# Two layers of a hybrid decoder on one core: another pacing of modulations and transposes, two heads' late rows in products of 512 and 256 columns, and another form of the last norm's factors

## The chip, the core and the metric

One Trainium2 chip, one of its cores. The time is what the device takes for one execution of the whole program, in microseconds; a kernel's time is the median of its runs. All weights come from the chip's own memory during the execution.

## What is computed

The reference, cut to what matters here. Two layers: a retention mixer (8 heads) with a SwiGLU feed-forward, then a short convolution mixer with a second SwiGLU, 256 tokens of width 2048, all in float32.

```python
for i in range(DEPTH):                                   # DEPTH = 2
    mod = (c_act @ w_mod[i] + b_mod[i])[:, None, :]      # one conditioning vector
    sh1, sc1, g1, sh2, sc2, g2 = jnp.split(mod, 6, axis=-1)
    h = rms_norm(x, norm1_g[i]) * (1.0 + sc1) + sh1
    y = retention_mixer(h, ...) if i == 0 else short_conv_mixer(h, ...)
    x = x + g1 * y
    h = rms_norm(x, norm2_g[i]) * (1.0 + sc2) + sh2
    x = x + g2 * swiglu(h, ffn_w_in[i], ffn_w_out[i])    # D_FF = 5632
return rms_norm(x, final_g)

def retention_mixer(h, cos, sin, w_in, w_out):
    q, k, v, g = jnp.split(h @ w_in, ...)                # q, k rotated by position
    o = rms_norm(chunked_gated_linear_attention(q, k, v, log_a))
    return (jax.nn.silu(g) * o) @ w_out
```

## The kernel before

**Products.** TensorE (PE) multiplies rounded operands. Each float32 weight tile is split in two rounded parts, `hi` (cast on ScalarE, ACT, L416) and `lo` (the rest, a subtraction on VectorE, DVE, L419), and so is each activation row. A product is then hi·hi + hi·lo + lo·hi. Three helpers write it out:

- `product` (L469, L472): weights stand still, and the activation's both parts, 512 columns, go past `hi`; a second matmul sends the rounded part, 256 columns, past `lo`. A result column group takes a whole bank of PSUM, with the two halves added later on DVE.
- `packed` (L531 to L533): the same in three matmuls of 256 columns, whose sum stands in half a bank.
- `thrice` (L482 to L484): activations stand still and the weights, 512 columns, go past, three matmuls for each 128 tokens. The retention values, the feed-forward's main part and, by `sevens`, a form of it with seven instead of eight block products use it.

**Weights.** One sequence of 1 MB pieces (`raw`) holds all weights in the order of use. `fetch` loads them (L377) into a ring of four buffers, which the modulation's pieces share (L315), on SyncE's queue (SP). `prepare` splits a piece; the parts go into five places of 1024 columns, so TensorE's weights are made some steps ahead of their use.

**Modulations.** A column of 128 values of `mod` is one multiply with a running sum on DVE over a 1 MB piece of `w_mod` (L323, at low priority), and a small step on GpSimd (POOL, L328 to L333). 160 of them are spread over the program by `paced`: after each step of the products it compares the count so far with the table `plan_mod`, whose pairs are (product units so far, modulations due by then). A unit is 128 rows by 128 columns of weights. Up to unit 2048 runs the retention with its output; up to 2688 the first feed-forward's first input part; up to 3008 its first output part; up to 3776 its second input part; 5184 is the end of the convolution mixer.

**Heads.** They run in the order 4, 0, 2, 1, 5, 3, 6, 7. Of some heads a part of the rows (`ks`) has already been multiplied in the start phase and is held in SBUF (`ahead`): of heads 0 and 1 the first ten of sixteen rows, of heads 2 and 3 the first thirteen. `pair(head, i)` makes q (i = 0), k (1) and the gate (2): the late rows go through `packed`, and L1111 adds the held part. Heads 5, 6 and 7 (`SIDE_BY_SIDE`) have nothing held and use `product` for q and k.

**Transposes.** A head's outputs are made while the next head's projections run: `mixed` leaves three steps (`outputs(0)`, `last_outputs`, `ends`) in a list, and `ticked` calls each after so many product units, by `STEPS`. `ends` transposes the normed outputs `o` (L1073) with TensorE (L1084).

**The gated units' banks.** After a group of sevens `mixed_sums` (L1208 to L1212) adds four banks of sums into SBUF; the next group of products waits for these banks.

**The end.** The last output products leave token-major banks; `added` multiplies by the gate, adds the residual and takes the sum of squares on ACT; `stored` finishes the final norm: the mean (L1446, DVE), the power −1/2 (L1450, POOL), the scaling (L1453 ACT, L1455 and L1457 DVE) and the stores (L1459).

**What sets the order.** TensorE's instructions stand as the program writes them. Those of DVE, ACT and POOL are put into one order for each engine by the framework's scheduler, by priorities, when the program is built; each engine then works its list off in that order and waits on semaphores.

Of the kernel before, what the change touches and what calls it, by code (L numbers as in the profile page):

```python
# [13 lines left out]
AF = mybir.ActivationFunctionType  # L14
# [3 lines left out]
P = 128  # L18
# [29 lines left out]
MOD_LEAD = 64  # L48
MOST = 0.08
MOD_PRIO = -300  # L50
STEPS = (8, 8, 20)
RAW_BUFS = 4
PLACES = 5
FETCHED, PLAIN, WARM, ADDED = 2, 3, (5, 0, 0, 0, 0, 0, 0, 8), ()
SIDE_BY_SIDE = (5, 6, 7)
LEFT, ENDS, EARLIER = 8, 2, 120

Q0, K0, V0, G0 = 0, HEADS * DK, 2 * HEADS * DK, 2 * HEADS * DK + HEADS * DV
# [203 lines left out]
def trunk(ctx: ExitStack, tc: tile.TileContext, x_in, c_in, pos_in, w_mod, cols_in, gain_in, tab_in, w_all, out):  # L262
# [12 lines left out]
    def tmp(tag, shape=(P, S), dtype=F32, pool=work, bufs=None):  # L275
        return pool.tile(list(shape), dtype, tag=tag, name=name(tag), bufs=bufs)
# [63 lines left out]
    todo.reverse()  # L340
    first = RET_SPANS[0].n * FIRST_KS
    early = sum(g.n * len(g.ks) for g in RET_SPANS)
    plan_mod = [(early, 0), (1024, 28), (1984, 72), (2688, 84), (3008, 96), (3776, 106), (5184, n_mod)]
    units, allowed = [0], [0.0]

    def paced(n):
# [112 lines left out]
    def product(g, act, base=0, before=None, banks=None, last=True):  # L459

        fresh = not banks
        banks = banks or [bank() for _ in g.cols]
        for k in g.ks:
            if before:
                before(k)
            h = act[k - base]
            for c, pt in zip(g.cols, banks):
                hi, lo = take(g, k, c)
                nc.tensor.matmul(  # L469
                    pt, hi, h, start=fresh and k == g.ks[0], stop=False, skip_group_check=True  # L470
                )
                nc.tensor.matmul(  # L472
                    pt[:, 1, :], lo, h[:, 0, :], start=False, stop=last and k == g.ks[-1], skip_group_check=True
                )
            ticked(len(g.cols))
            paced(len(g.cols))
        return banks
# [241 lines left out]
    with ExitStack() as inner:  # L719
# [374 lines left out]
        def pair(head, i):  # L1094

            g = RET_HEADS[head][0][i]
            if not g.ks:
                return [ahead[head, n] for n in ((i,) if i < 2 else (2, 3))]
            if i < 2 and head in SIDE_BY_SIDE:
                both = tmp("qs", (P, 2, S), pool=rp, bufs=1)  # L1100
                for j, pt in enumerate(product(g, h)):
                    summed(pt, both[:, j])
                return [both]
            sums = packed(g, h)
            for j, pt in enumerate(sums):
                key = (head, i + j)
                if key in tag_of:
                    free.append(tag_of.pop(key))
                if key in ahead:
                    s = tmp("qs", (P, 2, S), pool=rp, bufs=1)  # L1110
                    nc.vector.tensor_tensor(s, ahead[key], pt, op=ALU.add)  # L1111
                    sums[j] = s
            return sums
# [306 lines left out]
    def gated(t, c, v, priority):  # L1420

        xs = at(xt[t], c)
        with tc.high_priority(offset=priority):
            nc.vector.tensor_tensor(v, v, gate_of[c], op=ALU.mult)
            nc.vector.tensor_tensor(xs, xs, v, op=ALU.add)

    def added(t, c, pt, last):

        u, xs = tmp("u512", (P, DV), pool=mpool, bufs=3), at(xt[t], c)
        nc.vector.tensor_tensor(u, pt, gate_of[c], op=ALU.mult)  # L1430
        nc.vector.tensor_tensor(xs, xs, u, op=ALU.add)
        if not last:
            return
        nc.scalar.activation(u, xs, AF.Square, accum_out=total[:, t, c : c + 1])
        if c < 3:
            nc.vector.tensor_tensor(xs, xs, gain_of[c], op=ALU.mult)
        if c == 2:
            some = sums_of[:, t : t + 1]
            nc.gpsimd.tensor_tensor(some, total[:, t, 0:1], total[:, t, 1:2], op=ALU.add)
            nc.gpsimd.tensor_tensor(some, some, total[:, t, 2:3], op=ALU.add)  # L1440
            nc.gpsimd.tensor_scalar(some, some, 1.0 / D, EPS, op0=ALU.mult, op1=ALU.add)

    def stored(t):

        r = tmp("rs", (P, 2), bufs=4)[:, 0:1]
        nc.vector.tensor_scalar(  # L1446
            r, total[:, t, 3:4], 1.0 / D, sums_of[:, t : t + 1], op0=ALU.mult, op1=ALU.add
        )
        root = tmp("rs", (P, 2), bufs=4)[:, 0:1]
        nc.gpsimd.tensor_tensor(root, r, half[:, 0:1], op=ALU.pow)  # L1450
        for i in range(2):
            a, b = at(xt[t], 2 * i), at(xt[t], 2 * i + 1)
            nc.scalar.activation(a, a, AF.Identity, scale=root)  # L1453
            if i:
                nc.vector.scalar_tensor_tensor(b, b, root, gain_of[3], op0=ALU.mult, op1=ALU.mult)  # L1455
            else:
                nc.vector.tensor_scalar(b, b, root, None, op0=ALU.mult)  # L1457
            o = slice(2 * DV * i, 2 * DV * (i + 1))
            nc.sync.dma_start(out[t, :, o], xt[t][:, o])  # L1459

    def last_output(part, c, groups, act, base):
# [24 lines left out]
        for (t, j), v in extra.items():  # L1486
            gated(t, c + j, v, MOD_PRIO)
            if part:
                xs, n = at(xt[t], c + j), c + j
                nc.scalar.activation(v, xs, AF.Square, accum_out=total[:, t, n : n + 1])  # L1490
                nc.vector.tensor_tensor(xs, xs, gain_of[n], op=ALU.mult)

    for part in range(2):
# [53 lines left out]
```

## Time and profile before

| | |
|---|---|
| three runs | 2565.79, 2567.32, 2568.79 us |
| the profiled execution | 2568.4 us, its span 2566.6 us |
| granted TensorE clock in it | 0.998 |
| weights and tables loaded | 685.11 MB, 268 GB/s over the span |

The span goes from the first to the last instruction; the 1.8 us beside it lie around the program. In the rows a line number names the line of the code, `bank` is PSUM, `raw` a loaded piece, and a matmul of 128x512 has 512 columns going past. A matmul's time in a row is longer than the distance to the next one's start, since they overlap; what a matmul costs is read from the starts.

### The profile page before, as it was taken

Reading aid. Unit: us, or ns where it says so; the run is one execution under the profiler, and the core shown is the slowest. Engines: PE = TensorE matmul, PEld = TensorE weight load, DVE = VectorE, ACT = ScalarE, POOL = GpSimd, SP = SyncE. Lnnn points to the kernel's source line nnn. Section 1 sums busy time; section 2 is a strip of 40 time slices with the busy share of each in tenths; the row PEclk is TensorE's granted clock in tenths of the full one; section 3 lists DMA queues with packets and bytes.
Section 4 is the critical chain, followed back from the end, with each engine's and each line's share of the span. In section 5 each row is a group of like instructions: output and inputs, shape, how many; then the busy total and the mean of one; then the engine's idle time right before and its main releaser. Section 6 shows DMA issues by size and latency. Waiting matters only on the chain.

```text
span 2566.6 us, 34867 instructions
## 1 busy us (share of the span) xinstructions
PE 2543.9 (99%) x13330; PEld 2186.1 (85%) x13330; DVE 2334.6 (91%) x2925; ACT 1346.1 (52%) x1789; POOL 178.4 (7%) x232
## 2 busy tenths in 40 slices
PE   8999999999999999999999999999999999999998
PEld 6898888888889888888888898888998888888887
DVE  7989999898899999889999888888989999999988
ACT  5544443454456555345555454444565555555554
POOL 0000111011111010000000111000000000000001
PEclk9999999999999999999999999999999999999999
DMA  9987889888876667866668878878846465555653
GB/s 398 390 331 263 309 321 340 334 300 308 329 278 234 231 261 285 322 245 227 248 230 301 302 282 309 330 292 299 317 159 214 180 229 212 181 214 182 228 197 131
DMA packets 96696, 689.48 MB, mean 269 GB/s; under 512 B 10744, under 2 KB 12168, under 8 KB 13456
## 3 DMA queue, kind: packets, MB, share of 16 engines
q1 hardware_dynamic: 96528, 687.25, 72.1%
q8 instruction: 104, 1.70, 0.3%
q14 instruction: 64, 0.52, 0.1%
HBM read 685.11 MB, written 2.11 MB: 268 GB/s over the span
## 4 chain that ended last, share of the span: by engine, by line
PE 90%; DVE 6%; DMA 2%; issue 1%; ACT 1%; ACTq 0%; SPq 0%; POOLq 0%; POOL 0%; DVEq 0%
PE bank L469 20%; PE bank L482 17%; PE bank L484 17%; PE bank L483 17%; PE bank L472 11%; DVE lo L419 2%; DMA raw<-w_all 1%; PE bank L533 1%; PE bank L664 1%; PE bank L532 1%; PE bank L666 1%; PE bank L665 1%; PE bank L531 1%; DVE raw L795 1%; DVE raw L323 1%
## 5 line engine op out<-in xcount | busy, mean ns | idle before, releaser
L416 ACT CAST hi<-raw 128x1024 fp32r<-128x1024 f32 (+1 forms) x981 | 990.5, 1020 | 932.8 <-PE bank L484 361.8
L419 DVE TENSOR_TENSOR lo<-raw,hi 128x1024 fp32r<-128x1024 f32 (+1 forms) x981 | 1143.9, 1181 | 148.3 <-ACT hi L416 143.3
L482 PE MATMUL bank<-hi,h 128*128 128x512 f32 x1540 | 602.7, 391 | 1.1 <-DVE u L1212 1.0
L483 PE MATMUL bank<-lo,h 128*128 128x512 f32 x1540 | 600.9, 390 | 0.1
L484 PE MATMUL bank<-hi,h 128*128 128x512 f32 x1540 | 600.8, 390 | 0.0
L323 DVE SCALAR_TENSOR_TENSOR raw<-raw,cb 128x2048 f32<-128x2048 f32 x160 | 365.9, 2287 | 28.9 <-DMA raw<-w_mod 28.6
L484 PEld LDWEIGHTS bank<-hi,h 128*128 128x128 f32 x1540 | 289.3, 188 | 61.2
L482 PEld LDWEIGHTS bank<-hi,h 128*128 128x128 f32 x1540 | 289.5, 188 | 59.6 <-DVE u L1212 1.9
L483 PEld LDWEIGHTS bank<-lo,h 128*128 128x128 f32 x1540 | 289.6, 188 | 58.4 <-DVE lo L419 0.8
L469 PE MATMUL bank<-h,hi 128*128 128x512 f32 x928 | 323.0, 391 | 0.0
L469 PE MATMUL bank<-mid,hi 128*128 128x512 f32 x920 | 319.4, 390 | 0.0
L472 PE MATMUL bank<-h,lo 128*128 128x256 f32 x928 | 261.3, 282 | 0.0
L472 PE MATMUL bank<-mid,lo 128*128 128x256 f32 x920 | 259.6, 282 | 0.0
L469 PEld LDWEIGHTS bank<-h,hi 128*128 128x128 f32 x928 | 174.1, 188 | 36.9
L469 PEld LDWEIGHTS bank<-mid,hi 128*128 128x128 f32 x920 | 172.7, 188 | 35.8
L472 PEld LDWEIGHTS bank<-h,lo 128*128 128x128 f32 x928 | 175.7, 189 | 0.3
L472 PEld LDWEIGHTS bank<-mid,lo 128*128 128x128 f32 x920 | 174.2, 189 | 0.1
L469 PE MATMUL bank<-rm,hi 128*128 128x512 f32 x496 | 172.5, 391 | 0.0
L472 PE MATMUL bank<-rm,lo 128*128 128x256 f32 x496 | 140.0, 282 | 0.0
L482 PE MATMUL bank<-hi,mid 128*128 128x512 f32 x297 | 116.0, 391 | 0.0
L484 PE MATMUL bank<-hi,mid 128*128 128x512 f32 x297 | 115.9, 390 | 0.0
L483 PE MATMUL bank<-lo,mid 128*128 128x512 f32 x297 | 115.7, 390 | 0.0
(281 smaller groups left out, 3430.4 us busy)
## 6 DMA issues: line engine op xcount, KB each, us to landing
raw<-w_all SPq DMA_DIRECT2D x456, 1024.0 KB, 5.0
raw<-w_mod SPq DMA_DIRECT2D x192, 1024.0 KB, 6.3
x<-x_in SPq DMA_DIRECT2D x4, 512.0 KB, 5.4
out<-xt SPq DMA_DIRECT2D x4, 512.0 KB, 3.0
decay<-tab_in SPq DMA_DIRECT2D x8, 128.0 KB, 5.3
x<-gate_row SPq DMA_DIRECT2D x2, 512.0 KB, 4.8
last_gain<-gain_in SPq DMA_DIRECT2D x1, 1024.0 KB
cols<-cols_in SPq DMA_DIRECT2D x1, 152.0 KB, 8.2
```

Of the source, the lines that this page charges most:

```text
L323: nc.vector.scalar_tensor_tensor(raw, raw, 1.0, cb, op0=ALU.mult, op1=ALU.mult, accum_out=total)
L416: nc.scalar.copy(hi[:, o], raw[:, o])
L419: nc.vector.tensor_tensor(lo, raw, hi.bitcast(F32), op=ALU.subtract)
L469: nc.tensor.matmul(pt, hi, h, start=fresh and k == g.ks[0], stop=False, skip_group_check=True)
L472: nc.tensor.matmul(pt[:, 1, :], lo, h[:, 0, :], start=False, stop=last and k == g.ks[-1], skip_group_check=True)
L482: nc.tensor.matmul(o, hi, w_hi, start=first, stop=False)
L483: nc.tensor.matmul(o, hi, w_lo, start=False, stop=False)
L484: nc.tensor.matmul(o, lo, w_hi, start=False, stop=last)
L531: nc.tensor.matmul(pt, hi, h[:, 0, :], start=first, stop=False, skip_group_check=True)
L532: nc.tensor.matmul(pt, hi, h[:, 1, :], start=False, stop=False, skip_group_check=True)
L533: nc.tensor.matmul(pt, lo, h[:, 0, :], start=False, stop=last, skip_group_check=True)
L664: nc.tensor.matmul(pt, hi, high, start=k == 0, stop=False, skip_group_check=True)
```

## The change

```diff
-STEPS = (8, 8, 20)
+STEPS = (8, 8, 24)
-SIDE_BY_SIDE = (5, 6, 7)
+SIDE_BY_SIDE, HELD_SIDE_BY_SIDE = (5, 6, 7), (1, 3)
...
-    plan_mod = [(early, 0), (1024, 28), (1984, 72), (2688, 84), (3008, 96), (3776, 106), (5184, n_mod)]
+    plan_mod = [(early, 0), (1024, 28), (1984, 72), (2688, 80), (3008, 96), (3776, 102), (5184, n_mod)]
...
+            if i < 2 and head in HELD_SIDE_BY_SIDE:
+                key = (head, i)
+                both = tmp("qs", (P, 2, S), pool=rp, bufs=1)
+                pts = product(g, h)
+                for j, pt in enumerate(pts):
+                    nc.vector.tensor_tensor(both[:, j], ahead[key][:, j], pt[:, 0, :], op=ALU.add)
+                    nc.vector.tensor_tensor(both[:, j], both[:, j], pt[:, 1, :], op=ALU.add)
+                free.append(tag_of.pop(key))
+                return [both]
...
-        nc.scalar.activation(u, xs, AF.Square, accum_out=total[:, t, c : c + 1])
-        if c < 3:
-            nc.vector.tensor_tensor(xs, xs, gain_of[c], op=ALU.mult)
+        sq = tmp("u512", (P, DV), pool=mpool, bufs=3)
+        nc.scalar.activation(sq, xs, AF.Square, scale=D**-0.5, accum_out=total[:, t, c : c + 1])
+        dst = xs if c < 3 else u
+        nc.vector.tensor_tensor(dst, xs, gain_of[c], op=ALU.mult)
+        gained[t] = dst
...
-            nc.gpsimd.tensor_scalar(some, some, 1.0 / D, EPS, op0=ALU.mult, op1=ALU.add)
+            nc.gpsimd.tensor_scalar(some, some, EPS, None, op0=ALU.add)
...
-        r = tmp("rs", (P, 2), bufs=4)[:, 0:1]
-        nc.vector.tensor_scalar(
-            r, total[:, t, 3:4], 1.0 / D, sums_of[:, t : t + 1], op0=ALU.mult, op1=ALU.add
-        )
         root = tmp("rs", (P, 2), bufs=4)[:, 0:1]
-        nc.gpsimd.tensor_tensor(root, r, half[:, 0:1], op=ALU.pow)
+        nc.gpsimd.tensor_tensor(root, total[:, t, 3:4], sums_of[:, t : t + 1], op=ALU.add)
+        nc.gpsimd.tensor_tensor(root, root, half[:, 0:1], op=ALU.pow)
         for i in range(2):
             a, b = at(xt[t], 2 * i), at(xt[t], 2 * i + 1)
             nc.scalar.activation(a, a, AF.Identity, scale=root)
-            if i:
-                nc.vector.scalar_tensor_tensor(b, b, root, gain_of[3], op0=ALU.mult, op1=ALU.mult)
-            else:
-                nc.vector.tensor_scalar(b, b, root, None, op0=ALU.mult)
+            nc.vector.tensor_scalar(b, gained[t] if i else b, root, None, op0=ALU.mult)
...
-                nc.scalar.activation(v, xs, AF.Square, accum_out=total[:, t, n : n + 1])
+                nc.scalar.activation(v, xs, AF.Square, scale=D**-0.5, accum_out=total[:, t, n : n + 1])
```

So: the third step of a head's outputs comes 24 instead of 20 units after the second. q and k of heads 1 and 3 go through `product`. Four modulations leave the first feed-forward's first input part for its first output part, and four leave its second input part for what follows. The mean's 1/D goes into the squares' scale, the mean's last addition moves from DVE to POOL, and the gain of the last 512 columns is multiplied in beside the squares instead of together with the root. The number of matmuls falls by 36.

Three places in the engines' lists follow. The first is TensorE in head 2's values, where head 0's outputs are transposed (`o_2452` and `o_2454` are the first and last 128 tokens, `bank_2431` and `bank_2432` the values' sums); minus is before, plus the change.

```order
-L1084 MATMUL bank_2506<-tab,o_2452 128x128 x2
-L1084 MATMUL bank_2507<-tab,o_2452 128x128 x2
-L1084 MATMUL bank_2506<-tab,o_2454 128x128 x2
-L1084 MATMUL bank_2507<-tab,o_2454 128x128 x2
 L482 MATMUL bank_2431<-hi,h 128x512
 L483 MATMUL bank_2431<-lo,h 128x512
...
 L483 MATMUL bank_2432<-lo,h 128x512
 L484 MATMUL bank_2432<-hi,h 128x512
+L1084 MATMUL bank_2512<-tab,o_2452 128x128 x2
+L1084 MATMUL bank_2513<-tab,o_2452 128x128 x2
+L1084 MATMUL bank_2512<-tab,o_2454 128x128 x2
+L1084 MATMUL bank_2513<-tab,o_2454 128x128 x2
```

The eight transposes stand six matmuls of 512 columns later; DVE's rows that make the two `o` keep their order there.

The second is DVE at the end of the first feed-forward's second group of sevens, where the four banks are added up (L1209 to L1212 before, L1218 to L1221 in the change, the same statements). Before:

```order
L323 SCALAR_TENSOR_TENSOR raw_7864,msum_7866<-raw_7864,cb 128x2048
L419 TENSOR_TENSOR lo<-raw_7889,hi 128x1024 x2
L1209 TENSOR_TENSOR u_1015_7904<-bank_7734,extra_6720 128x512
L419 TENSOR_TENSOR lo<-raw_7911,hi 128x1024
L1210 TENSOR_TENSOR extra_6721<-bank_7735,u_1015_7904 128x512
L419 TENSOR_TENSOR lo<-raw_7911,hi 128x1024
L1211 TENSOR_TENSOR u_1016_7905<-bank_7733,extra_6721 128x512
L1212 TENSOR_TENSOR u_1015_7904<-bank_7733,u_1015_7904 128x512
```

And with the change:

```order
L419 TENSOR_TENSOR lo<-raw_7830,hi 128x1024 x2
L419 TENSOR_TENSOR lo<-raw_7848,hi 128x1024
L1218 TENSOR_TENSOR u_1010_7863<-bank_7700,extra_6693 128x512
L419 TENSOR_TENSOR lo<-raw_7848,hi 128x1024
L1219 TENSOR_TENSOR extra_6694<-bank_7701,u_1010_7863 128x512
L419 TENSOR_TENSOR lo<-raw_7870,hi 128x1024
L1220 TENSOR_TENSOR u_1011_7864<-bank_7699,extra_6694 128x512
L1221 TENSOR_TENSOR u_1010_7863<-bank_7699,u_1010_7863 128x512
```

No modulation stands ahead of the four additions any more, and one weight split less. Between the ends of the first and the second group's additions DVE's list has one L323 instead of two; up to the end of the first group's it has 75 instead of 77, at the fourth group's 79 instead of 83.

The third is DVE at the very end, for the last 128 tokens. Before:

```order
L1430 TENSOR_TENSOR u_2252_21043<-bank_20633,x_74 128x512
L1431 TENSOR_TENSOR xt_15854<-xt_15854,u_2252_21043 128x512
L1446 TENSOR_SCALAR rs_21047<-total,sums 128x1
L1457 TENSOR_SCALAR xt_15854<-xt_15854,rs_21049 128x512
L1455 SCALAR_TENSOR_TENSOR xt_15854<-xt_15854,rs_21049,last_gain 128x512
```

With the change:

```order
L1441 TENSOR_TENSOR u_2258_21026<-bank_20613,x_74 128x512
L1442 TENSOR_TENSOR xt_15834<-xt_15834,u_2258_21026 128x512
L1448 TENSOR_TENSOR u_2258_21026<-xt_15834,last_gain 128x512
L1464 TENSOR_SCALAR xt_15834<-xt_15834,rs_21032 128x512
L1464 TENSOR_SCALAR xt_15834<-u_2258_21026,rs_21032 128x512
```

The mean's step has left DVE, the gain's multiplication stands ahead of the wait for the root, and the step behind the root has one tensor less to read.

1 line of the change is left out of this document (added).

## The prediction

> **What bounds the kernel now.** I read the page's busy shares first, then the chain that ended last, then TensorE's own waits behind the start phase (from 200 us on).
>
> ```profile
> span 2566.6 us, 34867 instructions
> PE 2543.9 (99%) x13330; PEld 2186.1 (85%) x13330; DVE 2334.6 (91%) x2925; ACT 1346.1 (52%) x1789; POOL 178.4 (7%) x232
> PE bank L1084 <- DVE o L1073: 2.3, 2, 1.2
> PE bank L482 <- DVE u L1212: 1.0, 1, 1.0
> ```
>
> TensorE is busy for 99% of the span: it sets the time, and a change can shorten the span only by the matmuls it removes, by the moments in which TensorE waits, and by what stands behind the last matmul. VectorE at 91% is the second limit, and the two rows of waits (what waited for what: us, times, longest) say that it is the one TensorE waits for. There is little to win: 3.3 us in these two. A modelled matmul end hides a part of each, so below I read waits from the distance of starts.
>
> **Products of heads 1 and 3.** Head 1 has six late rows, head 3 three; with two column groups each for q and k that is 2 x 2 x (6 + 3) = 36 blocks, each three matmuls before and two now. The price of both forms stands in the timeline, here in `product` and then in `packed`:
>
> ```profile
> 440.12 0.39 PE L469 MATMUL bank<-rm,hi 128*128 128x512 f32 x1
> 440.47 0.39 PE L469 MATMUL bank<-rm,hi 128*128 128x512 f32 x1
> 309.55 0.28 PE L531 MATMUL bank<-h,hi 128*128 128x256 f32 x1
> 309.91 0.28 PE L531 MATMUL bank<-h,hi 128*128 128x256 f32 x1
> ```
>
> From L469 to L469 0.35 us, from L531 to L531 0.36 us: the columns are the same 768, and only the third start goes. With the rows' rounding the difference is 0 to 0.02; I take 0.01. 36 blocks: **−0.4 us**, bounds 0 and −0.7. The Trainium skill, "TensorE: Matmul & The Clock Gate", section "Wait — 56ns, not 53.3ns?", gives the distance of two matmuls as columns over 2.4 GHz plus some 2.5 ns, so a start less saves 2.5 ns and the term would be −0.1; by it a matmul of 256 columns takes 0.109, here the three take 0.36, 0.12 each, so the rows do not agree.
>
> VectorE pays for it: one addition of 512 columns becomes four of 256.
>
> ```profile
> L1111 DVE TENSOR_TENSOR qs<-rm,bank 128x512 f32<-128x512 f32 x16 | 11.0, 685 | 0.0
> L549 DVE TENSOR_TENSOR rm<-bank,rm 128x256 fp32r<-128x256 f32 x32 | 12.8, 421 | 0.0
> 320.00:520.00 200.00, 200.00 (x1064) 173.13 (x1064) 180.56 (x217) 87.32 (x111) 25.05 (x45) 1.00 0.88 327
> ```
>
> 4 x 0.421 − 0.685 = 1.0 us for each q and k, 4.0 us for two heads. The windows' row (PE, PEld, DVE, ACT, POOL) has VectorE idle for 200 − 180.6 = 19.4 us in these 200, and TensorE does not wait there. q and k are needed only behind the values' 64 units. I take 0; without that cover it would be +4.0.
>
> **Transposes 4 units later.** The wait of 2.3 us is one place, head 0's outputs in head 2's values:
>
> ```profile
> 282.81 2.29 DVE L323 SCALAR_TENSOR_TENSOR raw<-raw,cb 128x2048 f32<-128x2048 f32 x1
> 283.07 2.57 POOL L583 TENSOR_TENSOR rs<-rs,half 128x2 f32<-128x2 f32 x1 [6.13 <-DVE rs L581]
> 284.33 0.39 PE L484 MATMUL bank<-hi,h 128*128 128x512 f32 x1
> 285.01 0.39 PE L484 MATMUL bank<-hi,h 128*128 128x512 f32 x1
> 285.69 0.75 DVE L1073 SCALAR_TENSOR_TENSOR o<-bank,rs,sg 128x512 f32<-128x512 f32 x1
> 286.59 0.63 PE L1084 MATMUL bank<-tab,o 128*128 128x128 f32 x4 [1.19 <-DVE o L1073]
> 287.55 0.75 DVE L1073 SCALAR_TENSOR_TENSOR o<-bank,rs,sg 128x512 f32<-128x512 f32 x1
> 288.35 0.66 PE L1084 MATMUL bank<-tab,o 128*128 128x128 f32 x4 [1.14 <-DVE o L1073]
> ```
>
> Three starts lie between the two L484, 0.227 us each. The first transposes could have started that much behind the second L484, at 285.24; they start at 286.59, 1.35 later. Four of them take some 0.45, and the second set starts at 288.35 instead of 287.04, another 1.31. With the change six matmuls of 0.227 go ahead, 1.36 us: the first set is reached at 286.60, when the first `o` is there, and the second at about 287.05, when the second is not: it is made at 287.55 by VectorE, whose list is the same here. So one wait of two goes: **−1.35 us**, bounds 0 (VectorE moves by as much) and −2.66 (both go).
>
> **Four modulations out of the first input part.** It runs from 823 to 1001 us and its waits stand at the ends of the groups, where the next group needs the banks that VectorE adds up.
>
> ```profile
> 823.00:1001.00 178.00, 176.84 (x796) 144.95 (x795) 175.98 (x222) 101.75 (x125) 15.82 (x13) 1.00 0.66 244
> PEld bank L483 <- DVE lo L419: 0.8, 2, 0.5
> 866.55 0.39 PE L484 MATMUL bank<-hi,h 128*128 128x512 f32 x1
> 867.03 0.50 PE L482 MATMUL bank<-hi,h 128*128 128x512 f32 x1
> 901.11 0.59 ACT L1208 COPY extra<-bank 128x512 f32<-128x512 f32 x1 [0.91 <-PE bank L484]
> 901.67 2.28 DVE L323 SCALAR_TENSOR_TENSOR raw<-raw,cb 128x2048 f32<-128x2048 f32 x1
> 906.15 0.68 DVE L1209 TENSOR_TENSOR u<-bank,extra 128x512 f32<-128x512 f32 x1
> 909.56 0.39 PE L484 MATMUL bank<-hi,h 128*128 128x512 f32 x1
> 910.95 0.50 PE L482 MATMUL bank<-hi,h 128*128 128x512 f32 x1 [1.00 <-DVE u L1212]
> 911.28 0.39 PE L483 MATMUL bank<-lo,h 128*128 128x512 f32 x1
> ```
>
> VectorE is idle here for 2 us of 178. The banks' copy is done at 901.7, but the additions begin at 906.15, behind a modulation of 2.28 us and two splits; TensorE's step from 909.56 to 910.95 is 1.39 instead of 0.23, and the next 0.33 instead of 0.23: 1.27 lost. At 867.03 it is 0.48 instead of 0.23 and, by the other's measure, 0.1 behind it: 0.35. The weight loads' waits (first row behind the window) have two more for a late split of weights, 0.8 us; they lie at the first group's start. In the changed list no modulation stands ahead of or among the additions of either group, so each chain should come some 2.28 us earlier, more than its wait; I count both, 1.6, and 0.3 of the 0.8, because there one modulation less stands ahead but the differences' step (L403) has come ahead too: **−1.9 us**, bounds 0 and −2.4.
>
> The four go where VectorE has more room:
>
> ```profile
> 1001.00:1114.00 113.00, 113.00 (x644) 99.86 (x643) 97.11 (x108) 43.71 (x44) 9.81 (x13) 1.00 0.83 307
> 1114.00:1368.00 254.00, 254.00 (x1148) 210.12 (x1147) 242.48 (x270) 143.49 (x162) 9.96 (x9) 1.00 0.65 236
> 1368.00:1503.00 135.00, 135.00 (x826) 121.62 (x825) 118.54 (x147) 63.77 (x82) 22.52 (x26) 1.00 0.83 308
> ```
>
> Four more of 2.28 are 9.1 us on 15.9 idle, and 4 MB in 113 us are 37 GB/s on 307, where the retention's row above ran at 327 without a wait. The other four go behind 1368, 16.5 idle in the first 135 us alone, and the second input part (1114 to 1368), where TensorE has no wait, gains nothing. I take 0; if nothing hid the first four, +9.1.
>
> **The end.** Behind the last matmul stands a chain. L1455 here is the first 128 tokens' last step, L1440 an addition ahead of it; the other rows are the last 128 tokens'.
>
> ```profile
> 2557.24 0.74 DVE L1455 SCALAR_TENSOR_TENSOR xt<-xt,rs,last_gain 128x512 f32<-128x512 f32 x1
> 2557.32 0.39 PE L484 MATMUL bank<-hi,mid 128*128 128x512 f32 x1
> 2557.90 0.69 DVE L1430 TENSOR_TENSOR u<-bank,x 128x512 f32<-128x512 f32 x1
> 2559.94 0.19 ACT L1434 ACTIVATION_READ_ACCUMULATOR u<-xt 128x1 f32 x1
> 2560.16 0.21 DVE L1446 TENSOR_SCALAR rs<-total,sums 128x1 f32<-128x1 f32 x1 [0.85 <-ACT u L1434]
> 2560.52 0.55 POOL L1450 TENSOR_TENSOR rs<-rs,half 128x1 f32<-128x1 f32 x1 [3.72 <-DVE rs L1446]
> 2561.11 1.34 ACT L1453 ACTIVATE xt<-xt,rs 128x512 f32<-128x512 f32 x2 [0.98 <-POOL rs L1450]
> 2553.11 0.19 POOL L1440 TENSOR_TENSOR sums<-sums,total 128x1 f32<-128x1 f32 x1
> ```
>
> The addition on POOL costs 0.19 where L1446 cost 0.21, with hand-overs alike: nothing from there. L1455 ends at 2557.98 and L1430 stands behind it, while the last matmul is modelled to end at 2557.71; L1455 becomes a shorter step, so L1430 can begin some 0.15 us earlier. Behind the root ACT's two steps of 1.34 end last, not VectorE's, so the shorter step there is hidden. The new gain step runs beside the squares. **−0.15 us**, bounds −0.4 and +0.5. In the bounds is what 283.07 shows: POOL's power took 2.57 us while VectorE's L323 ran, against 0.55 alone. The Trainium skill, "GPSIMD Engine Reference", "1. Specifications", says that POOL shares its SBUF interfaces with VectorE's instructions of two SBUF inputs, and L323 agrees; the new gain step is one such, but by these rows it ends 0.1 to 0.2 us ahead of POOL's start.
>
> **Sum.** −0.4 − 1.35 − 1.9 − 0.15 = −3.8 us: 2568.4 of the profiled execution, of which the span is 2566.6, becomes 2564.6. The runs' median is 2567.3, so it becomes **2563.5 us**, 0.15% less. About 0.2%, 5.1 us, is what a measurement of this kernel can tell from no change.
>
> **The rivals.**
>
> *All of the waits go.* If VectorE's second `o` also comes in time, and the late splits go too, the sum is −0.7 − 2.66 − 2.4 − 0.15 = −5.9: 2561.4. For it: VectorE has up to 2.28 us less to do in a group. Against it: VectorE's list at the second `o` is unchanged.
>
> *The waits move.* VectorE is idle for 2 us in 178 at the first input part; if its backlog is an older one, the additions are late all the same, and only products, the end and half the transposes' wait remain: −0.4 − 0.15 − 0.7 = −1.3, 2566.0. For it: the third and fourth groups have as many modulations before and show no wait, so their number alone does not decide. Against: the 2.28 us of the quoted one stand right ahead of the additions.
>
> *Slower: the first output part is overfilled.* Sixteen modulations in 113 us hold the ring's four buffers longer, weights come late and the five places run empty. It decides from the point at which VectorE's 97.1 + 9.1 = 106.2 us of 113 no longer fit between the steps that TensorE needs; then the 9.1 are paid: 2563.5 + 9.1 = 2572.6. Against it: 6.8 us of 113 are left, 6%, and the second input part has 11.5 of 254, under 5%, without a wait of TensorE.
>
> **How the numbers follow.** Forecast 0.58, all waits go 0.20, waits move 0.14, slower 0.08. Faster by over 0.2% (under 2562.2): nearly all of the first rival and a seventh of the forecast, 0.27. Slower by over 0.2% (over 2572.4): most of the third, 0.06. The rest, 0.67, within. The range holds the forecast, the first two rivals and a run's spread of 1.5 us: 2560.2 to 2568.0.
>
> **What would show it.** TensorE's waits for `o` fall from 2.3 to about 1.2, with one of two left near 288 us; the wait for L1212 is gone; L531 and L469 have 36 blocks exchanged at 0.35 instead of 0.36 us; VectorE is busier from 1001 to 1114 with TensorE still without a wait; the scaling behind the last root begins some 3.8 us earlier than 2561.1, and all but 0.15 of it is there at the last matmul. A wait of TensorE between 1001 and 1114 us, or one of `o` as long as before, would make it wrong.

## The result, and the profile after

The changed kernel took 2562.49 us (median of 22 runs, 2562.16 to 2566.94), the kernel before 2566.64 us in 22 runs of the same comparison (2565.35 to 2568.79): a ratio of 0.9986, 95% interval 0.998 to 0.9992, so faster by 0.14%, less than the 0.2% that one measurement of this kernel tells from no change. A second comparison gave 0.9987, 0.9978 to 0.9996; both intervals lie below 1. The forecast was 2563.5 us. Much of the spread within a kernel goes with the clock granted over the whole run: in the comparisons of this document the kernel before has a median of 2565.87 us in its 65 runs with a granted clock of 0.998 or more and 2567.76 in its 37 with 0.997, the changed kernel 2562.43 (24 runs) and 2564.93 (9 runs).

The changed kernel's profiled execution has a span of 2560.6 us, 6.0 less than before's. First its span and TensorE's share, then TensorE's waits from 200 us to the end (what waited for what: us, times, longest):

```profile
span 2560.6 us, 34823 instructions
PE 2541.4 (99%) x13294; PEld 2182.2 (85%) x13294; DVE 2338.6 (91%) x2937; ACT 1345.4 (53%) x1789; POOL 178.1 (7%) x234
```

```profile
PE bank L1064 <- DVE sp L549: 0.5, 1, 0.5
```

The waits for `o` and for the banks are gone; one for a head's `sp`, which before has as well, is left. At head 0's transposes the timeline (start, us, engine, line) now reads:

```profile
282.87 0.74 DVE L1073 SCALAR_TENSOR_TENSOR o<-bank,rs,sg 128x512 f32<-128x512 f32 x1
284.73 0.74 DVE L1073 SCALAR_TENSOR_TENSOR o<-bank,rs,sg 128x512 f32<-128x512 f32 x1
286.06 1.03 PE L1084 MATMUL bank<-tab,o 128*128 128x128 f32 x8
```

All eight transposes go through in one piece, and the second `o` is there 0.6 us ahead of the first of them. Before, VectorE began these two at 285.69 and 287.55, each 2.8 us later, while TensorE was only 0.5 us later: VectorE's time there was not the same, though its list was. At the end of the first feed-forward's second group:

```profile
897.14 0.58 ACT L1217 COPY extra<-bank 128x512 f32<-128x512 f32 x1
898.40 0.69 DVE L1218 TENSOR_TENSOR u<-bank,extra 128x512 f32<-128x512 f32 x1
902.47 0.68 DVE L1221 TENSOR_TENSOR u<-bank,u 128x512 f32<-128x512 f32 x1
```

The additions begin 1.26 us after the banks' copy instead of some 5 and are over at 903.2. The windows of the first input part and of the first output part (PE, PEld, DVE, ACT, POOL, granted clock, DMA share, GB/s):

```profile
823.00:1001.00 178.00, 178.00 (x813) 147.39 (x813) 172.70 (x209) 101.46 (x122) 15.70 (x11) 1.00 0.62 225
1001.00:1114.00 113.00, 113.00 (x636) 99.40 (x635) 98.01 (x109) 42.66 (x42) 9.35 (x18) 1.00 0.90 335
```

VectorE has 5.3 us of room in the first input part instead of 2, and TensorE is without a pause. In the first output part VectorE's work rises from 97.1 us to 98.0 only, where the prediction added 9.1. Over the same work (the changed kernel stands 5.6 us earlier there, so 995.4 to 1108.4 us) L323 takes 38.95 us instead of 29.83, but VectorE's sum is 98.7: other work left as the modulations came. Behind the last matmul:

```profile
2551.51 0.39 PE L484 MATMUL bank<-hi,mid 128*128 128x512 f32 x1
2551.93 0.69 DVE L1441 TENSOR_TENSOR u<-bank,x 128x512 f32<-128x512 f32 x1
2553.39 0.69 DVE L1448 TENSOR_TENSOR u<-xt,last_gain 128x512 f32<-128x512 f32 x1
2553.98 0.19 ACT L1446 ACTIVATION_READ_ACCUMULATOR u<-xt 128x1 f32 x1
2554.24 0.19 POOL L1459 TENSOR_TENSOR rs<-total,sums 128x1 f32<-128x1 f32 x1 [3.14 <-ACT u L1446]
2554.51 0.56 POOL L1460 TENSOR_TENSOR rs<-rs,half 128x1 f32<-128x1 f32 x1
2555.11 1.33 ACT L1463 ACTIVATE xt<-xt,rs 128x512 f32<-128x512 f32 x2 [0.94 <-POOL rs L1460]
```

From the last matmul's start to the accumulator's read 2.47 us instead of 2.62, from there to the scaling 1.13 instead of 1.17.

Where the time went, worked out from TensorE's starts in two executions of each kernel (the second ones are the experiments before_again and after_again below), in us:

| stretch | before | before, again | changed | changed, again |
|---|---|---|---|---|
| start, to the first L1064 | 229.90 | 229.29 | 229.36 | 229.58 |
| to the 19th L1064 (head 0's transposes in it) | 80.73 | 78.44 | 77.93 | 77.91 |
| to the first L664 (the other heads) | 464.91 | 464.90 | 464.79 | 464.79 |
| to the 17th transpose of units, 962 us | 187.01 | 187.02 | 184.91 | 184.91 |
| to the 33rd, 1159 us | 196.41 | 196.41 | 196.19 | 196.19 |
| to the last matmul | 1398.36 | 1398.27 | 1398.33 | 1398.27 |
| to the end of the span | 9.29 | 9.29 | 9.12 | 9.13 |
| span | 2566.6 | 2563.6 | 2560.6 | 2560.8 |

The feed-forward's gain is the same in both pairs, 2.32 and 2.33. That at head 0 is 2.8 in the first and 0.5 in the second.

### The profile page after: what moved, and what is told of

It is laid out like the page before. It is cut to its first block, busy times and chain, and to the rows that moved or that the text cites. A ratio compares the mean times of both kernels' runs of the same rounds, so it can differ in the third digit from the quotient of the medians.

```text
span 2560.6 us, 34823 instructions
## 1 busy us (share of the span) xinstructions
PE 2541.4 (99%) x13294; PEld 2182.2 (85%) x13294; DVE 2338.6 (91%) x2937; ACT 1345.4 (53%) x1789; POOL 178.1 (7%) x234
## 4 chain that ended last, share of the span: by engine, by line
PE 95%; DVE 2%; DMA 1%; ACT 1%; issue 0%; POOL 0%; SPq 0%; ACTq 0%; POOLq 0%; DVEq 0%
PE bank L469 21%; PE bank L482 18%; PE bank L484 18%; PE bank L483 18%; PE bank L472 11%; PE bank L664 1%; PE bank L666 1%; PE bank L665 1%; PE bank L533 1%; PE bank L532 1%; PE bank L531 1%; DVE raw L795 1%; DMA raw<-w_all 1%; PE bank L1287 1%; PE bank L1064 1%; DMA raw<-w_mod 1%
## 5 line engine op out<-in xcount | busy, mean ns | idle before, releaser
L484 PE MATMUL bank<-hi,h 128*128 128x512 f32 x1540 | 600.3, 390 | 0.0
L323 DVE SCALAR_TENSOR_TENSOR raw<-raw,cb 128x2048 f32<-128x2048 f32 x160 | 365.1, 2283 | 11.5 <-DMA raw<-w_mod 11.1
L484 PEld LDWEIGHTS bank<-hi,h 128*128 128x128 f32 x1540 | 289.1, 188 | 61.3
L469 PE MATMUL bank<-h,hi 128*128 128x512 f32 x964 | 336.0, 392 | 0.0
L472 PE MATMUL bank<-h,lo 128*128 128x256 f32 x964 | 271.2, 281 | 0.0
L469 PEld LDWEIGHTS bank<-h,hi 128*128 128x128 f32 x964 | 180.9, 188 | 38.9
L472 PEld LDWEIGHTS bank<-h,lo 128*128 128x128 f32 x964 | 182.1, 189 | 0.5
L484 PE MATMUL bank<-hi,mid 128*128 128x512 f32 x297 | 115.8, 390 | 0.0
```

What stands on the lines that cost most here:

```text
L323: nc.vector.scalar_tensor_tensor(raw, raw, 1.0, cb, op0=ALU.mult, op1=ALU.mult, accum_out=total)
L469: nc.tensor.matmul(pt, hi, h, start=fresh and k == g.ks[0], stop=False, skip_group_check=True)
L472: nc.tensor.matmul(pt[:, 1, :], lo, h[:, 0, :], start=False, stop=last and k == g.ks[-1], skip_group_check=True)
L484: nc.tensor.matmul(o, lo, w_hi, start=False, stop=last)
```

## The experiments

Each was built from one of the two kernels. The intervals of single parts are some ±0.1%, 2.3 us, so the medians alone settle few of them; the traces do.

### Each part alone, on the kernel before

**The transposes alone:**

```diff
-STEPS = (8, 8, 20)
+STEPS = (8, 8, 24)
```

> The kernel before with STEPS = (8, 8, 24) alone. The prediction's theory: one of TensorE's two waits for `o` at head 0's transposes goes, -1.35 us, the second stays near 288 us with about 1.1 us. Rival A, what the changed kernel's trace shows: both waits go with this edit alone, -2.7 us. Rival B: VectorE's lead of 2.8 us there in the changed kernel was one execution's loading and not the edit: then the second wait is here in one profile and not in another, and the median falls by 1.3 to 2.7. Rival C, the waits move: VectorE's next work is late by as much and the time falls by 0 to 0.5 us. In every case the starts of TensorE behind 330 us stand earlier by that amount than before's.

Measured: 2567.11 us against 2566.11, ratio 1.0003 (0.9994 to 1.0012). The waits for `o` are gone, as Rival A has it, and TensorE stands 3.25 us ahead of before's first trace at 775 us (0.34 ahead of before_again's); at 962 us it is only 0.6 ahead. ScalarE's row there in the timeline, and then TensorE's waits from 823 to 1001 us:

```profile
896.14 2.52 ACT L416 CAST hi<-raw 128x1024 fp32r<-128x1024 f32 x3 [3.56 <-DMA raw<-w_all]
```

```profile
PE bank L482 <- DVE u L1212: 1.4, 1, 1.4
PE bank L482 <- DVE extra L1210: 1.4, 1, 1.4
PE bank L483 <- DVE lo L419: 0.3, 1, 0.3
```

A weight piece issued at 888.57 took 7.5 us to land; in s4_end, which has the same first feed-forward, the same piece took 5.4 and there was one wait instead of two. So in this trace the gain at the heads was lost again at the next place where VectorE is full, by a late load; l2_no_plan below, with the same STEPS and the same table, had the piece after 4.7 us and has one wait there. The median of 1.0 above before's need not be the part's doing: six of these eleven runs had a granted clock of 0.996 or 0.997, but only 10 of before's 33. The other five have a median of 2565.32, before's other 23 one of 2565.78, so 0.5 less, about what the traces give for the transposes.

**The modulations' table alone:**

```diff
-... (2688, 84), (3008, 96), (3776, 106), ...
+... (2688, 80), (3008, 96), (3776, 102), ...
```

> The kernel before with the new table of modulations alone (80 by 2688, 102 by 3776). The prediction's theory: the ends of the first feed-forward's first two groups lose 1.6 us of bank waits and 0.3 us of late splits, -1.9 us, with nothing paid from 1001 to 1114 us or later. What the changed kernel's trace shows: -2.4 us between 823 and 1001. Rival, the waits move: 0 to -0.5, a new wait at a later group's end or in the first output part. Rival, overfilled: +1 us or more between 1001 and 1114. Median 2564.2 to 2565.0 if the theory holds and before stands at 2566.6.

Measured: 2564.99 against 2566.11, 0.9993 (0.9984 to 1.0002). The stretch to 962 us is 184.87 instead of 187.01 and the next one 196.19 instead of 196.41: -2.36 us, no wait of TensorE from 823 to 1001 us and none later. The theory holds with a term a little above the forecast's 1.9.

**The products alone** (the new branch of `pair` as in the change):

```diff
-SIDE_BY_SIDE = (5, 6, 7)
+SIDE_BY_SIDE, HELD_SIDE_BY_SIDE = (5, 6, 7), (1, 3)
```

> The kernel before with q and k of heads 1 and 3 through `product` alone, 36 matmuls fewer. The prediction's theory: -0.4 us (bounds 0 and -0.7), all of it between 300 and 560 us, VectorE's 4.0 us more of additions hidden. The spacing of the two traces (120 ns for each of three matmuls, 228 + 118 for the two) gives 36 x 13.5 ns = -0.5. Rival: the additions stand in front of something that TensorE waits for, +1 to +4 us, seen as a wait of TensorE for the scores' sums or for `o` in heads 1, 5 or 6. By the medians alone this is not to be told from nothing; the starts of TensorE in one profile tell it.

Measured: 2567.89 against 2566.11, 1.0006 (0.9998 to 1.0015). The matmuls of q and k of both heads take 0.25 us less, but this trace has four places that are worse than before_again, +0.7 and +0.4 at the transposes, +0.3 at the banks and +0.4 near 999 us, 1.8 together (L1109 and L1110 are the new additions; the timeline of the second of the four):

```profile
520.72 0.42 DVE L1110 TENSOR_TENSOR qs<-qs,bank 128x256 f32<-128x256 f32 x1
521.04 0.42 DVE L1109 TENSOR_TENSOR qs<-rm,bank 128x256 f32<-128x256 f32 x1
521.33 0.60 PE L1084 MATMUL bank<-tab,o 128*128 128x128 f32 x4
521.38 0.75 DVE L1073 SCALAR_TENSOR_TENSOR o<-bank,rs,sg 128x512 f32<-128x512 f32 x1
522.18 0.66 PE L1084 MATMUL bank<-tab,o 128*128 128x128 f32 x4 [0.25 <-DVE o L1073]
```

The additions stand ahead of the second `o`, which comes 0.4 us late. That is the one place where the rival is shown: VectorE's 4.0 us more are not free on the old pacing. The 0.7 at head 0's transposes is not theirs, since it comes at 286 us, ahead of the first new product at some 304 us; there a weight piece landed late (the table of landings below). What made the other two places, 350 us and more behind the last new product, is not shown.

**The end alone** (`added`, `stored` and the squares as in the change; two of its lines):

```diff
-        nc.gpsimd.tensor_tensor(root, r, half[:, 0:1], op=ALU.pow)
+        nc.gpsimd.tensor_tensor(root, total[:, t, 3:4], sums_of[:, t : t + 1], op=ALU.add)
+        nc.gpsimd.tensor_tensor(root, root, half[:, 0:1], op=ALU.pow)
```

> The kernel before with the last norm's factors put as in the change, and nothing else. The prediction's theory: -0.15 us (bounds -0.4 and +0.5), all behind the last matmul; in the two traces the stretch from the last matmul's start to the span's end is 9.28 us before and 9.09 in the change, so -0.2 is expected. Rival: POOL's addition and power run beside VectorE's new gain step and are slowed, +0.5 us or more between the accumulator's read and ACT's scaling.

Measured: 2566.88 against 2566.11, 1.0003 (0.9994 to 1.0012). From the last matmul's start to the end 9.12 us against 9.29 in both traces of before. The power takes 0.56 as before, so the rival falls.

### Both kernels again, and each part left out of the changed one

**The changed kernel, unedited:**

> The changed kernel once more, on the chip of the three kernels that each leave one part of it out. If the changed kernel's first trace shows the kernel and not one lucky execution, TensorE has again no wait for `o` behind 260 us and none for the banks between 823 and 1001 us, and the median lies 3.5 to 4.5 us under before's. If before's trace was the unusual one (its piece issued at 270.81 us took 9.0 us to land, the same piece 7.2 and 4.9 us in the traces of the single parts), the difference is smaller, 2 to 3 us.

Measured: 2562.57 against 2566.22, 0.9987 (0.9978 to 0.9996); no wait for `o` or for the banks in this trace either.

**The kernel before, unedited:**

> The kernel before once more, for a second trace of it. Theory: the 2.65 us of waits for `o` near 286 us in its first trace belong to that one execution, which ran 1.8 us above its kernel's median, because a weight piece landed late; the traces of the plan's part and of the end's part, whose code is the same up to there, lost 0.4 us. Then this trace shows 0.3 to 1 us of waits for `o`, and the bank waits between 823 and 912 us are there as before, 1.7 us or more by the starts. Rival, the edits of the single parts took the wait away: 2.2 to 2.7 us again.

Measured: 2565.40 us in its one run, 1.9 under the median of before's first three. The theory holds. In before's first trace the piece issued at 270.81 has, in the view of its tile, the line

```profile
DMA to landing us min/median/max: 9.0/9.0/9.0
```

and the timeline then has ScalarE's wait for it and VectorE's for ScalarE:

```profile
279.92 1.05 ACT L416 CAST hi<-raw 128x1024 fp32r<-128x1024 f32 x1 [4.10 <-DMA raw<-w_all]
281.00 1.23 DVE L419 TENSOR_TENSOR lo<-raw,hi 128x1024 fp32r<-128x1024 f32 x1 [1.98 <-ACT hi L416]
```

In before_again the same piece, issued at 270.20, has

```profile
DMA to landing us min/median/max: 5.1/5.1/5.1
```

and the timeline the same two steps, 3 us earlier and with no wait for the load, and behind them the second `o` and its transposes:

```profile
276.69 1.06 ACT L416 CAST hi<-raw 128x1024 fp32r<-128x1024 f32 x1 [1.47 <-PE bank L484]
278.11 1.21 DVE L419 TENSOR_TENSOR lo<-raw,hi 128x1024 fp32r<-128x1024 f32 x1
...
284.66 0.74 DVE L1073 SCALAR_TENSOR_TENSOR o<-bank,rs,sg 128x512 f32<-128x512 f32 x1
285.46 0.66 PE L1084 MATMUL bank<-tab,o 128*128 128x128 f32 x4 [0.22 <-DVE o L1073]
```

The same program, the same 1 MB: landed after 9.0 us in one execution, after 5.1 in the other, and VectorE's pause of 2 us there is most of what TensorE then waits for. Twelve traces share this place; the time the piece took, and what TensorE's steps at the eight transposes lost:

| STEPS[2] | trace: landing us -> lost us |
|---|---|
| 20 | before 9.0 -> 2.65; s3_products 7.4 -> 1.05; l1_no_steps 7.0 -> 0.67; before_again 5.1, s4_end 4.9, s2_plan 4.9 -> 0.39 each |
| 24 | w_burst 7.8 -> 0.30; l3_no_products 7.7 -> 0.46; s1_steps 7.2 -> 0; changed 5.0, after_again 5.0, l2_no_plan 4.8 -> 0 |

With 20 the wait is the longer the later the piece; with 24 three late pieces left 0 to 0.46. Four units more are worth 0.4 us where the piece lands after 5 us, and where it lands after 7 to 8 us they leave at most 0.5 of some 1 us.

**The changed kernel without the transposes' part:**

```diff
-STEPS = (8, 8, 24)
+STEPS = (8, 8, 20)
```

> The changed kernel with STEPS back at 20. If the transposes' four units are worth what before's trace shows, it is 2.7 us slower than the changed kernel; by the traces of the single parts, where the same code waited 0.4 and 1.5 us in place of 2.65, it is 0.4 to 1.5 us slower, with waits for `o` near 286 us and perhaps 522 us. The prediction's 1.35 lies inside the second. Rival: no difference, since VectorE gives the time back later.

Measured: 2563.89 against 2566.22, 0.9991 (0.9983 to 1.0), 1.3 above after_again by the medians. By the starts 0.67 us are lost at head 0 and 0.41 near 523 us, 1.08 together, inside the second figure. The place near 523 is the one that s3_products showed; with 24 it is covered.

**The changed kernel without the new table:**

```diff
-... (2688, 80), (3008, 96), (3776, 102), ...
+... (2688, 84), (3008, 96), (3776, 106), ...
```

> The changed kernel with the old table of modulations. Theory: the first input part is where TensorE and VectorE meet; without the four modulations taken out, whatever TensorE gained ahead of it is given back there, as in the trace of the transposes' part alone (3.3 us ahead at 775 us, 0.6 at 962). Then it is 2.5 to 5 us slower than the changed kernel and hardly faster than before, with waits for L1221 and L1219 between 863 and 912 us. Rival, the parts add up: 1.9 to 2.3 us slower.

Measured: 2565.46 against 2566.22, 0.9997 (0.9988 to 1.0006), 2.9 slower than after_again by the medians and 2.83 by the starts from 775 to 1159 us, of it 1.5 at this wait (the modelled end of the matmul ahead hides a part of it):

```profile
PE bank L482 <- DVE u L1221: 1.4, 1, 1.4
```

That is 0.47 more than the same edit gave alone (2.36), at the lower edge of the theory. Counted from the first L1064, this kernel is 0.63 us ahead of before_again at 775 us and 0.14 ahead at 1159: most of what TensorE gained ahead of the first input part is given back in it, as the expectation has it. So the table is worth its 2.36 alone, and 0.5 more because without it the other parts' gain does not last.

**The changed kernel without the products' part:**

```diff
-SIDE_BY_SIDE, HELD_SIDE_BY_SIDE = (5, 6, 7), (1, 3)
+SIDE_BY_SIDE, HELD_SIDE_BY_SIDE = (5, 6, 7), ()
```

> The changed kernel without heads 1 and 3 through `product` (packed again, 36 matmuls more, 4.0 us less work for VectorE). Theory: 0.4 to 0.5 us slower. Rival, VectorE's additions are not free: the trace of this part alone showed waits of 1.0 and 0.4 us for `o` and 1.5 us at the banks, more than in its neighbours, and a median 1.8 us above before's (interval 0.9998 to 1.0015); then this kernel is 0 to 1.5 us faster than the changed one. In the trace the matmuls of head 1's q and k take 24 x 13.5 ns = 0.3 us more, those of head 3's 0.16.

Measured: 2564.85 against 2566.22, 0.9992 (0.9983 to 1.0001). By the medians it is 2.3 slower than after_again, but nine of its eleven runs had a granted clock of 0.997, against three of after_again's; the other two have 2562.42 and 2562.92, after_again's other eight a median of 2562.28. In its trace 2 us lie ahead of the first L1064 (last section); from there on it is 0.8 us slower than after_again, 0.46 of it the late piece of the table above and 0.25 the matmuls. So inside the changed kernel `product` gains its quarter and VectorE's additions are hidden; the rival falls.

### How far the pacing can be pushed

**A head's outputs 4 units later, on the changed kernel:**

```diff
-STEPS = (8, 8, 24)
+STEPS = (12, 8, 24)
```

> The changed kernel with STEPS = (12, 8, 24): the scores' sums of a head are used 4 units later, and everything behind them. Every trace so far has TensorE wait about 1.0 us near 230 us for `sp` (two steps 0.2 and 0.67 late, two more 0.1 each), the only wait that the changed kernel still has behind 200 us. Theory: the wait goes and nothing takes its place, -0.8 to -1.0 us, 2561.6; it would beat both kernels. Rival, it moves: VectorE's own next work is as late, 0 to -0.3. Rival, later outputs hold banks and buffers longer, +0.5 us or more with a new wait at a head's gate or at the next head's scores.

Measured: 2561.56 us (2561.07 to 2563.65) against 2567.43, 0.998 (0.9972 to 0.9989). The changed kernel's last wait,

```profile
230.60 0.50 PE L1064 MATMUL bank<-v,sp 128*128 128x512 f32 x1 [0.50 <-DVE sp L549]
```

is gone, and no engine is named in TensorE's list of waits behind 200 us any more. Its median is 0.9 under the changed kernel's 2562.5 in two comparisons: it beats both kernels. The intervals against before overlap, but the runs with a granted clock of 0.998 or more do not: six here from 2561.07 to 2561.56, and 24 of the changed kernel from 2562.08 to 2563.72.

**Eight more modulations in the first output part, on the changed kernel:**

```diff
-... (2688, 80), (3008, 96), (3776, 102), ...
+... (2688, 72), (3008, 96), (3776, 102), ...
```

> The changed kernel with the first feed-forward's first input part holding eight modulations less again, so 24 in place of 16 in its first output part of 113 us. Theory: VectorE has 98.0 of 113 us there in the changed kernel; 8 x 2.28 = 18.2 more are 116, over what there is, so TensorE waits there or the modulations spill into the second input part: +1 to +4 us, with waits between 1001 and 1130 us. Rival: the list spreads them without a wait and the time is that of the changed kernel, 2562.5.

Measured: 2572.36 us (2570.63 to 2573.93), 1.0021 (1.0012 to 1.003): 9.8 us slower than the changed kernel. 7.4 of it are in the stretch from 962 to 1159 us. The window of the first output part, then ScalarE's waits in it, then TensorE's from 1001 to 1130 us:

```profile
1001.00:1114.00 113.00, 110.21 (x618) 95.78 (x617) 104.49 (x112) 36.18 (x36) 18.91 (x30) 1.00 0.98 371
```

```profile
ACT hi L416 <- DMA raw<-w_all: 66.4, 16, 6.6
ACT hi L416 <- DVE raw L323: 4.9, 1, 4.9
```

```profile
PE bank L472 <- DVE lo L419: 2.7, 4, 0.9
PE bank L483 <- DVE lo L419: 1.2, 1, 1.2
```

More than the expectation's 1 to 4, and not by VectorE's time: it is busy for 104.5 of 113 us and has room, but ScalarE waits 66 us for weight pieces, 25 in the changed kernel. The pieces issued in this window were not slower from issue to landing, 7.0 us in the median against 6.8 in the changed kernel; fewer of them were weights. Of 41 pieces 22 are `w_mod`'s and 19 weights, in the changed kernel 14 and 21 of 35, and SyncE waits 33.2 us instead of 14.9 for L323 to free a buffer before it issues a piece of `w_mod`. So by this trace the eight more pieces take the weights' turns in the ring of four buffers that both share. The DMA engines' share rises with it, from 0.90 to 0.98; whether a longer ring would have helped at that share was not tested.

**The pause of the start filled, on w_steps0:**

```diff
-... WARM, ADDED = 2, 3, (5, 0, 0, 0, 0, 0, 0, 8), ()
+... WARM, ADDED = 2, 3, (5, 0, 0, 0, 0, 12, 0, 8), ()
```

> The changed kernel with STEPS = (12, 8, 24) and twelve more matmuls of ones (24 instructions, no part of the result) in the 3.49 us near 13 to 16.5 us in which TensorE waits for POOL's power. In the traces so far the granted clock from 16 to 25 us is 1.00 in five, 0.81 in four and 0.62 to 0.67 in the others, and the start stands up to 3.4 us later where it is low; every kernel's runs lie in two groups some 2 to 3 us apart. Theory: the low clock follows that pause, so with the pause filled the clock is 1.00 there, the later of the two groups of runs goes, and the runs lie between 2561.0 and 2561.9 with a median near 2561.3 (w_steps0: 2561.07 to 2563.65). Rival, the groups have another cause (a late weight piece): the same two groups again. Rival, the added matmuls end after 16.5 us and hold up the next product: all runs 0.3 to 1 us later.

Measured: 2561.72 us (2561.27 to 2562.52) against 2566.01, 0.9982 (0.9973 to 0.9991). The later group of runs is gone, the spread is 1.25 us instead of 2.58, but the median is 0.2 above that of w_steps0 and not below it, and the expected range, 2561.0 to 2561.9, is passed at its upper end. All eleven runs have a granted clock of 0.999; w_steps0's six runs at 0.998 or more have a median of 2561.32, 0.4 lower, and why is not shown. The clock's side of it stands in the last section.

## Why the forecast came out as it did

**The products, forecast -0.4.** The step "I take 0.01" from rows of 0.35 and 0.36 was rounding. Head 1's q in s1_steps, which keeps `packed`, first and eighth block:

```profile
304.48 0.28 PE L531 MATMUL bank<-h,hi 128*128 128x256 f32 x1
306.99 0.28 PE L531 MATMUL bank<-h,hi 128*128 128x256 f32 x1
```

and in the changed kernel:

```profile
304.47 0.39 PE L469 MATMUL bank<-h,hi 128*128 128x512 f32 x1
306.93 0.40 PE L469 MATMUL bank<-h,hi 128*128 128x512 f32 x1
```

Seven blocks in 2.51 and 2.46 us: 7 ns each, and 36 of them give -0.25, which is also what both heads' q and k show. The mechanism was right, the size was off by less than a half. That VectorE's 4.0 us are free is right only in company: with 20 units in STEPS (s3_products, l1_no_steps) they cost 0.4 us near 522 us.

**The transposes, forecast -1.35.** Here a step failed: "the second at about 287.05, when the second is not: it is made at 287.55 by VectorE, whose list is the same here". The list was the same, its time was not. It was set by when one weight piece landed, and before's profiled execution had the latest of twelve. The first pair of traces shows -2.65, the usual execution -0.4, plus 0.4 near 523 us that the new products would have cost; -1.35 lies between by chance, as does the 1.3 by the medians of l1_no_steps.

**The first input part, forecast -1.9.** Right in place and cause: both groups' additions come early, and the waits at these two groups' ends go in every trace with the new table and in none with the old. The size is 2.33: 1.27 in the second group, as counted, 0.84 instead of 0.65 in the first, and 0.22 near 1000 us, where the fourth group's units wait in before, was not counted. The four modulations' new place cost nothing, as forecast, with the DMA engines at 0.90.

**The end, forecast -0.15.** -0.17 and -0.16 in the two pairs. The 0.15 ahead of the accumulator's read came as worked out; the hand-over through POOL is 0.04 shorter instead of equal. One reading was off without harm: the 2.57 us of POOL's power beside L323 are for 128x2 values, and the 0.55 beside them for 128x1; the eleven powers of 128x2 in before have a median of 0.71.

**The sum.** With the second trace of both, 0.25 + 0.39 + 2.33 + 0.16 less 0.29 of a later start is 2.8, the difference of the two second spans (2563.6 and 2560.8). The medians differ by 3.65 and 4.15; the forecast has 3.8. The clock does not make the rest: among the runs with a granted clock of 0.998 or more the medians still differ by 3.4. That the rest is late pieces, which the kernel before pays for and the changed one mostly does not, fits the table of landings, where the six traces with 20 lost 0.92 us on average, 0.53 more than before_again; but it was not shown run by run, since a run without a profile does not tell where it waited. That the sum came so near is in part luck: the first input part was counted 0.4 too low, and the transposes' term comes near what the medians of l1_no_steps give, though the second wait that it leaves standing is gone in both traces of the changed kernel.

**The rivals.** "All of the waits go" describes the first pair of traces: -5.9 forecast, -6.0 measured, 0.5 of it the start. "The waits move" did not happen in the changed kernel, but where the old table stays: 0.5 us in l2_no_plan, more in s1_steps' trace with its late piece. "Overfilled" needed 24 modulations and not 16. Its path is the one that w_burst shows, the ring's buffers held and the weights late; its condition, VectorE's time, is not, since that still had room. Its price of 9.1 us, for four modulations, was near the 9.8 measured for eight more, by chance.

## What to carry to other kernels

One trace gives a wait's place and cause, not its size: where the wait ends at an engine that follows a load, take a second trace, or ask how late that load could be, before pricing the cure. A part that costs a full engine work (the products) can lose at one place what another part (the later transposes) covers there. When work is moved into a stretch with idle time, ask about the buffers that its loads share as well as the engine's time: 16 pieces fitted beside the weights, 24 did not, with VectorE at 104.5 of 113 us. And before two medians are compared, compare the granted clocks of their runs: s1_steps is 1.0 us slower than before by the medians and 0.5 faster by the runs of 0.998 and more, l3_no_products 2.3 slower than after_again and 0.4.

## What the chip showed that was not expected

**A pause of 3.5 us costs the clock, by chance.** In the start phase TensorE waits for POOL's power. The windows from 16 to 25 us (granted clock is the third number from the right) of the kernel before, the changed kernel, w_steps0 and w_warm, in this order:

```profile
16.00:25.00 9.00, 8.57 (x38) 7.16 (x39) 8.10 (x10) 2.69 (x8) 0.37 (x1) 0.81 1.01 422
```

```profile
16.00:25.00 9.00, 8.27 (x42) 6.47 (x43) 8.13 (x10) 2.72 (x8) 0.40 (x1) 1.00 1.01 422
```

```profile
16.00:25.00 9.00, 7.90 (x31) 7.02 (x32) 8.17 (x11) 2.44 (x6) 1.05 (x1) 0.62 1.02 424
```

```profile
16.00:25.00 9.00, 8.72 (x43) 6.68 (x44) 7.64 (x10) 2.29 (x6) 0.00 (x0) 1.00 1.01 423
```

Of the thirteen traces without the filled pause four have 1.00 (not five, as the expectation counted), four 0.81 and five 0.62 to 0.67, whatever the kernel. At half clock, 0.81 over 9 us is 3.4 us of it and 0.62 is 6.8, one and two times the same length, and the first L515 stands at 21.1 us in the changed kernel, 22.1 in before and 24.2 in l3_no_products, which has 0.62. By 95 us this is made good: the first L531 behind the same row of L484 starts at 94.33 in the changed kernel and at 94.12 in l3_no_products. The 2.3 us by which l3_no_products is later at the first L1064 (231.62 against 229.36) are lost near 107 us. In four of the five traces with 0.62 to 0.67 (not in s4_end) TensorE waits there for 1.8 to 2.4 us, in all the others for 1.3, and the clock is at half once more behind the longer wait. l3_no_products, with its window, and then the changed kernel, each with the L531 that stands eighteen matmuls behind the wait:

```profile
107.78 0.39 PE L531 MATMUL bank<-h,hi 128*128 128x256 f32 x1 [2.22 <-ACT h L823]
112.58 0.28 PE L531 MATMUL bank<-h,hi 128*128 128x256 f32 x1
108.00:112.00 4.00, 3.93 (x16) 3.47 (x16) 3.48 (x5) 2.57 (x3) 0.00 (x0) 0.58 1.01 420
```

```profile
107.06 0.38 PE L531 MATMUL bank<-h,hi 128*128 128x256 f32 x1 [1.29 <-ACT h L823]
110.32 0.28 PE L531 MATMUL bank<-h,hi 128*128 128x256 f32 x1
```

These four are also the only traces whose granted clock over the whole run is 0.997. Why the longer wait follows only some of the slow starts was not tested. In w_warm the first pause is 0.81 us long, and the later of the two groups of runs is gone:

```profile
15.98 0.71 PE L590 MATMUL bank<-tab,rs 128*128 128x128 f32 x4 [0.81 <-POOL rs L922]
16.53 1.95 PE L863 MATMUL bank<-ones 128*128 128x128 f32 x16
```

The Trainium skill, "TensorE: Matmul & The Clock Gate", section "What's actually happening", has the clock set by a free-running window of 3.4 us, with half clock after an idle one. The traces agree in the length of the stretches and in that the same pause of 3.49 us is followed sometimes by none, sometimes by one and sometimes by two of them. They do not show that a whole window must be idle: near 107 us waits of 1.8 to 2.4 us were followed by half clock, those of 1.3 were not.

**The same transfer differs by 4 us.** A piece of 1 MB, issued at the same place of the same list, landed after 4.8 to 9.0 us in twelve executions. This kernel's TensorE is busy for 99% of the span, and head 0's transposes show what such a delay costs it where there is no cover.
